# Gate and up products of two feed-forward layers by Strassen's algorithm, with down products in five steps between the pairs

## Chip, cores and metric

One Trainium2 chip, one core of it. The metric is the device time of one execution in microseconds; the kernel before takes 1113.04 us (median of 3 runs, 1112.74 to 1113.41).

## What is computed

A decoder layer in float32 for 512 tokens of width 1024: a feed-forward layer, a token mixer with two kinds of attention, a second feed-forward layer, a last normalisation. The change concerns the feed-forward layers alone:

```python
def swiglu(x, w_gate, w_up, w_down):
    return (jax.nn.silu(x @ w_gate) * (x @ w_up)) @ w_down

x = x + 0.5 * swiglu(rms_norm(x, ffn1_norm), ffn1_w_gate, ffn1_w_up, ffn1_w_down)
...
x = x + 0.5 * swiglu(rms_norm(x, ffn2_norm), ffn2_w_gate, ffn2_w_up, ffn2_w_down)
```

The inner width is 2816, which is 22 blocks of 128.

## The kernel before

Activations lie transposed: 8 tiles of 128 channels by 512 tokens. To keep float32 accuracy, every operand of a product is split in a high part (rounded to the matmul's format by a cast on ScalarE, `whi`) and a low part (what is left, by a subtraction on VectorE, `wlo`). A product then takes three matmuls for each 128 channels: low weights by high activations, high by high, high weights by low activations (`mm3`, L109 to L112). `split` (L98 to L104) makes the two parts of a block of weights in three rotating buffers each; `load` (L92) brings a block on SP's queue into two rotating buffers of 1 MB (`wraw`).

`ffn_up` (L310) goes through the 22 inner blocks. For each it makes a gate and an up product, `gemm` (L114): 8 channel tiles x 3 matmuls with 512 tokens each, into one PSUM bank. `finish` (L313) multiplies both by the row factors of the norm (`Rb`), applies silu on ScalarE, multiplies, and splits the result in `hh` and `hl`. All 22 pairs are kept. The down product of the first layer (L381 to L394) comes after the last block: for four pairs of output tiles, over all 22 blocks. That of the second (L930 to L932, with tokens on the output's partitions) also follows after all blocks, into all eight banks at once. Rotary tables (`rope_table`, L354) are made beside five steps of the first layer and stay in SBUF.

Within an engine, instructions run in the order that the program has; this order is set by a scheduler from the program's dependences, except at the very start. TensorE does its steps in the order of the code.

Of the kernel before, what the change touches and what calls it, by code (L numbers as in the profile page):

```python
# [56 lines left out]
def hybrid_layer_kernel(ctx: ExitStack, tc: tile.TileContext, x, positions,  # L57
# [11 lines left out]
    wraw = ctx.enter_context(tc.tile_pool(name="wraw", bufs=2))  # L69
# [16 lines left out]
    cmask = const.tile([P, T], F32, name="cmask")  # L86
    pool.memset(cmask, 0.0)
    pool.affine_select(out=cmask[:, T - P:T], in_=cmask[:, T - P:T], compare_op=ALU.is_ge, fill=-BIG,
                       base=0, pattern=[[-1, P]], channel_multiplier=1)

# [1 line left out]
    def load(view, eng=None):  # L92
        _, a, b = view.shape
        t = wraw.tile([P, a, b], F32, name="raw", tag="raw")
        (eng or nc.sync).dma_start(out=t, in_=view)
        return t
# [98 lines left out]
    xgp = xg_stack.enter_context(tc.tile_pool(name="xgp", bufs=KT))  # L195
    ffn1_stack = ExitStack()
    xpool = ffn1_stack.enter_context(tc.tile_pool(name="xpool", bufs=1))
    work = ffn1_stack.enter_context(tc.tile_pool(name="work", bufs=2))
    xt = [xpool.tile([P, T], F32, name=f"xt{k}") for k in range(KT)]

    def gain_split(src, gain):
        xh = xgp.tile([P, T], F32R, name="xh", tag="xh")
        xl = xgp.tile([P, T], F32R, name="xl", tag="xl")
        act.activation(xh, src, AF.Copy, scale=gain)
        vec.scalar_tensor_tensor(out=xl, in0=src, scalar=gain, in1=as_f32(xh), op0=ALU.mult, op1=ALU.subtract)
        return xh, xl
# [5 lines left out]
    tbl = ExitStack()  # L212
    tcs = tbl.enter_context(tc.tile_pool(name="tcs", bufs=1, side="right"))
    tbl_a = ExitStack()
    tqk = tbl_a.enter_context(tc.tile_pool(name="tqk", bufs=1, side="right"))

    with tc.tile_pool(name="xnat", bufs=1) as xnp:
# [11 lines left out]
        # keeps the tensor engine's clock up until the first operands are there  # L229
        warm = xnp.tile([P, T], BF16, name="warm")  # L230
        vec.memset(warm, 0.0)
        with tc.manual_schedule(engines={EN.PE, EN.Activation, EN.DVE}):
            ps_first = [bank(), bank()]
            first_w = [[xnp.tile([P, KT, P], F32R, name=f"first_{n}{j}") for n in ("hi", "lo")] for j in range(2)]
            xg = []
# [13 lines left out]
            def split_x(*ks):  # L249
                for k in ks:  # L250
                    xg.append(gain_split(tps[k], gain("ffn1", k)))
# [9 lines left out]
            def keep_x(*ks):  # L261
                for k in ks:
                    act.copy(xt[k], tps[k])
# [37 lines left out]
    def sumsq_add(work, acc, k, src):  # L301
        if k == 0:
            vec.tensor_tensor(out=acc, in0=src, in1=src, op=ALU.mult)
        else:
            sq = work.tile([P, T], F32, name="sq", tag="sq")
# [4 lines left out]
    def ffn_up(work, hp, w_gate, w_up, xg, r, first=None, extra=None):  # L310
        hs = []

        def finish(ps_g, ps_u):  # L313
            g = work.tile([P, T], F32, name="g", tag="g")
            u = work.tile([P, T], F32, name="u", tag="u")
            vec.tensor_tensor(out=g, in0=ps_g, in1=Rb, op=ALU.mult)  # L316
            act.activation(g, g, AF.Silu)
            vec.tensor_tensor(out=u, in0=ps_u, in1=Rb, op=ALU.mult)  # L318
            vec.scalar_tensor_tensor(out=g, in0=g, scalar=0.5, in1=u, op0=ALU.mult, op1=ALU.mult)
            hh = hp.tile([P, T], F32R, name="hh", tag="hh")  # L320
            hl = hp.tile([P, T], F32R, name="hl", tag="hl")
            act.copy(hh, g)
            vec.tensor_tensor(out=hl, in0=g, in1=as_f32(hh), op=ALU.subtract)
            hs.append((hh, hl))

        f = 0 if first is None else 1
        while f < FT:
            if extra is not None:
                extra(f)
            n = 1 if f % 2 else 2  # L330
            raw_g = load(kview(w_gate, f * P, (f + n) * P))
            raw_u = load(kview(w_up, f * P, (f + n) * P))
            for s in range(n):
                ps_g, ps_u = (bank("tp"), bank("sc")) if (f + s) % 2 else (bank(), bank())
                gemm(ps_g, split(raw_g[:, :, s * P:(s + 1) * P]), kcols, xg)
                if r is not None:
                    set_R(r)
                    r = None
                gemm(ps_u, split(raw_u[:, :, s * P:(s + 1) * P]), kcols, xg)
                if first is not None:  # L340
                    finish(*first)
                    first = None
                finish(ps_g, ps_u)
            f += n
        return hs

# [1 line left out]
    rc = const.tile([P, 20], F32, name="rc")  # L348
    pool.dma_start(out=rc, in_=rope_const)
    tables = [(tqk if j < 3 else tcs).tile([P, T], F32, name=f"table{j}") for j in range(5)]  # L350
    t_even, t_odd, t_kr, t_cos, t_sin = tables

    # rotary tables, one for each of a few steps of the first layer
    def rope_table(f):  # L354
        j = f // 2 - 2
        if f % 2 or not 0 <= j < 5:
            return
        c = rc[:, 4 * j:4 * j + 4]
        t = tables[j]
        pos = work.tile([P, T], I32, name="pos", tag="sq")  # L360
        pool.dma_start(out=pos, in_=positions[0].partition_broadcast(P))
        a = work.tile([P, T], F32, name="ang", tag="g")
        kk = work.tile([P, T], F32, name="kk", tag="u")
# [9 lines left out]
        act.activation(t, a, AF.Sin)  # L373
        vec.tensor_scalar(out=t, in0=t, scalar1=c[:, 2:3], scalar2=c[:, 3:4], op0=ALU.mult, op1=ALU.add)

    with tc.tile_pool(name="h1", bufs=FT) as hp:
        hs = ffn_up(work, hp, ffn1_w_gate, ffn1_w_up, xg, r0, ps_first, rope_table)
        xg = []
        acc = work.tile([P, T], F32, name="acc", tag="u")
        wd = ffn1_w_down[0].rearrange("(a p) n -> p a n", p=P)  # L380
        for n2 in range(KT // 2):  # L381
            pss = [bank(), bank()]
            for f0, f1 in ((0, 8), (8, 16), (16, 22)):
                raw = load(wd[:, f0:f1, n2 * 256:(n2 + 1) * 256])
                for s in range(2):
                    wh, wl = split(raw[:, :, s * P:(s + 1) * P])
                    for f in range(f0, f1):
                        mm3(pss[s], wh[:, f - f0, :], wl[:, f - f0, :], hs[f][0], hs[f][1], f == 0, f == FT - 1)
            for s in range(2):
                k = n2 * 2 + s  # L390
                vec.tensor_tensor(out=xt[k], in0=xt[k], in1=pss[s], op=ALU.add)
                pool.dma_start(out=x1d[k], in_=xt[k])
                xg.append(gain_split(xt[k], gain("mix", k)))
                sumsq_add(work, acc, k, xt[k])  # L394
# [6 lines left out]
    off = dict(cq=0, ckv=256, kr=384, dq=416, dk=928, dv=1440, gm=1952, gd=2976)  # L401
    mix = ExitStack()
# [44 lines left out]
    # decoupled key: columns [key, swapped key] in high parts, then in low parts  # L447
# [19 lines left out]
    # sums the four row groups and repeats the sum in each  # L467
# [17 lines left out]
    # differential values, put by in DRAM  # L485
# [16 lines left out]
    # minus lambda  # L502
# [543 lines left out]
```

## Time and profile before

| what | value |
|---|---|
| runs | 1112.74, 1113.04, 1113.41 us |
| profiled execution: span from its first to its last instruction | 1111.0 us |
| TensorE busy, share of the span | 1097.5 us, 99% |
| VectorE busy | 608.0 us, 55% |
| ScalarE busy | 414.1 us, 37% |
| moved by DMA | 130.10 MB, mean 117 GB/s |

The profile is that of one execution. What the runs have above its span (2.0 us for their median) lies before its first and after its last instruction, together with the spread of the runs. A busy time is the time in which an engine has at least one instruction; matmuls overlap each other, so 99% says that TensorE has work nearly always, not how fast it goes through it.

### The profile page before, as it was taken

How to read it: one execution, taken by the hardware profiler on the slowest of the kernel's cores; microseconds unless marked ns; L12 is line 12 of the kernel's file. 1: busy time of each engine (PE TensorE's matmuls, PEld its weight loads, DVE VectorE, ACT ScalarE, POOL GpSimd, SP SyncE). 2: the span in 40 equal slices, each digit the busy share in tenths (PEclk: the TensorE clock that was granted, in tenths of full speed). 3: DMA queues.
4: the chain of work that ended last, by engine and by line, in shares of the span. 5: the costliest groups of instructions: out<-in, count | busy, mean ns of one | idle time of the engine just before them, and what ended most of it. 6: DMA issues, size and time to landing. Idle time of an engine off the chain costs nothing.

```text
span 1111.0 us, 12841 instructions
## 1 busy us (share of the span) xinstructions
PE 1097.5 (99%) x4972; PEld 898.0 (81%) x4972; DVE 608.0 (55%) x1143; ACT 414.1 (37%) x710; POOL 43.4 (4%) x48
## 2 busy tenths in 40 slices
PE   8999999999999999999999999999999999999997
PEld 6888888888888887888777788888888888888885
DVE  5666654442333567998488868554444444432223
ACT  5433333331222334666455534433222333221124
POOL 2000000000000100022000000000000000000003
PEclk9999999999999999999999999999999999999999
DMA  7324323323323415442766247333223323323221
GB/s 220 106 92 130 107 76 102 125 77 105 121 93 119 123 48 152 119 128 81 254 198 188 87 148 235 119 95 114 76 81 125 99 76 111 116 95 114 76 76 76
DMA packets 112174, 130.10 MB, mean 117 GB/s; under 512 B 4038, under 2 KB 95344, under 8 KB 112112
## 3 DMA queue, kind: packets, MB, share of 16 engines
q1 hardware_dynamic: 103664, 111.32, 31.3%
q10 hardware_dynamic: 6944, 13.87, 3.8%
q0 software_dynamic: 1504, 4.09, 1.2%
q8 instruction: 39, 0.64, 0.2%
q14 instruction: 23, 0.19, 0.0%
HBM read 113.01 MB, written 15.73 MB: 116 GB/s over the span
## 4 chain that ended last, share of the span: by engine, by line
PE 96%; DVE 2%; DMA 1%; ACT 0%; issue 0%; SPq 0%; DVEq 0%; ACTq 0%
PE bank_gb L110 18%; PE bank_gb L112 18%; PE bank_gb L111 18%; PE bank_sc L112 4%; PE bank_sc L111 4%; PE bank_sc L110 4%; PE bank_tp L110 4%; PE bank_tp L111 4%; PE bank_tp L112 4%; PE bank_sc L930 1%; PE bank_sc L932 1%; PE bank_sc L931 1%; PE bank_sc L767 1%; PE bank_gb L930 1%; PE bank_tp L932 1%; PE bank_tp L930 1%
## 5 line engine op out<-in xcount | busy, mean ns | idle before, releaser
L102 ACT CAST whi<-raw 128x1024 fp32r<-128x1024 f32 (+1 forms) x183 | 183.8, 1006 | 514.5 <-PE bank_gb L112 271.6
L103 DVE TENSOR_TENSOR wlo<-raw,whi 128x1024 fp32r<-128x1024 f32 (+1 forms) x175 | 203.3, 1162 | 151.2 <-ACT whi L102 150.5
L110 PE MATMUL bank_gb<-xh,wlo 128*128 128x512 f32 x544 | 218.4, 401 | 0.0
L112 PE MATMUL bank_gb<-xl,whi 128*128 128x512 f32 x544 | 213.5, 392 | 0.0
L111 PE MATMUL bank_gb<-xh,whi 128*128 128x512 f32 x544 | 212.7, 391 | 0.0
L110 PEld LDWEIGHTS bank_gb<-xh,wlo 128*128 128x128 f32 x544 | 102.5, 188 | 23.3 <-issue 3.0
L112 PEld LDWEIGHTS bank_gb<-xl,whi 128*128 128x128 f32 x544 | 102.4, 188 | 22.3 <-issue 0.4
L111 PEld LDWEIGHTS bank_gb<-xh,whi 128*128 128x128 f32 x544 | 102.6, 189 | 19.3
L110 PE MATMUL bank_tp<-xh,wlo 128*128 128x512 f32 x184 | 71.8, 390 | 0.0
L111 PE MATMUL bank_tp<-xh,whi 128*128 128x512 f32 x184 | 71.6, 389 | 0.0
L112 PE MATMUL bank_tp<-xl,whi 128*128 128x512 f32 x184 | 71.6, 389 | 0.0
L110 PE MATMUL bank_sc<-xh,wlo 128*128 128x512 f32 x176 | 68.6, 390 | 0.0
L112 PE MATMUL bank_sc<-xl,whi 128*128 128x512 f32 x176 | 68.5, 389 | 0.0
L112 PE MATMUL bank_gb<-hl,whi 128*128 128x512 f32 x176 | 68.5, 389 | 0.0
L110 PE MATMUL bank_gb<-hh,wlo 128*128 128x512 f32 x176 | 68.5, 389 | 0.0
L111 PE MATMUL bank_sc<-xh,whi 128*128 128x512 f32 x176 | 68.5, 389 | 0.0
L111 PE MATMUL bank_gb<-hh,whi 128*128 128x512 f32 x176 | 68.5, 389 | 0.0
L318 DVE TENSOR_TENSOR u<-bank_sc,Rb 128x512 f32<-128x512 f32 x22 | 15.2, 691 | 63.1 <-PE bank_sc L112 63.1
L318 DVE TENSOR_TENSOR u<-bank_gb,Rb 128x512 f32<-128x512 f32 x22 | 15.2, 691 | 56.6 <-PE bank_gb L112 56.6
L589 DVE CUSTOM_DVE_ANT_0 bank_sc<-bank_sc,cmask 128x128 f32<-128x128 f32 (+3 forms) x64 | 31.5, 496 | 18.1 <-PE bank_sc L767 17.4
L316 DVE TENSOR_TENSOR g<-bank_tp,Rb 128x512 f32<-128x512 f32 x22 | 15.2, 691 | 46.8 <-PE bank_tp L112 46.8
L112 PEld LDWEIGHTS bank_tp<-xl,whi 128*128 128x128 f32 x184 | 34.6, 188 | 7.2
(396 smaller groups left out, 1845.3 us busy)
## 6 DMA issues: line engine op xcount, KB each, us to landing
raw<-in_ffn_w_gate_dram SPq DMA_DIRECT2D x21, 1024.0 KB
raw<-in_ffn_w_up_dram SPq DMA_DIRECT2D x21, 1024.0 KB
raw<-in_ffn_w_down_dram SPq DMA_DIRECT2D x19, 1024.0 KB
raw<-in_w_in_dram SPq DMA_DIRECT2D x11, 1024.0 KB
raw<-in_w_in_dram SPq DMA_DIRECT2D x8, 512.0 KB
raw<-in_w_out_dram SPq DMA_DIRECT2D x4, 1024.0 KB
raw<-in_ffn_w_down_dram SPq DMA_DIRECT2D x4, 768.0 KB
xn<-in_x_dram SPq DMA_DIRECT2D x4, 512.0 KB
```

The source lines that it names most:

```text
L102: act.copy(hi, src)
L103: (eng or vec).tensor_tensor(out=lo, in0=src, in1=as_f32(hi), op=ALU.subtract)
L110: pe.matmul(ps, wl, xh, start=start, stop=False)
L111: pe.matmul(ps, wh, xh, start=False, stop=False)
L112: pe.matmul(ps, wh, xl, start=False, stop=stop)
L316: vec.tensor_tensor(out=g, in0=ps_g, in1=Rb, op=ALU.mult)
L318: vec.tensor_tensor(out=u, in0=ps_u, in1=Rb, op=ALU.mult)
L589: vec.tensor_tensor_reduce(out=ps[:, 0:n], in0=ps[:, 0:n], in1=cmask[:, T - n:T], op0=ALU.add, op1=ALU.min, scale=-scale, scalar=3e38, acc ...
L767: pe.matmul(ps[:, 0:n], qa[rs, s, qs], kl[rs, 0:n], start=False, stop=True)
L930: pe.matmul(ps, hh[:, ts], wl[:, cs], start=first, stop=False)
L931: pe.matmul(ps, hh[:, ts], wh[:, cs], start=False, stop=False)
L932: pe.matmul(ps, hl[:, ts], wh[:, cs], start=False, stop=(f == FT - 1))
```

## The change

The first two pairs of inner blocks (four blocks) stay as they were. For the other nine pairs, `strassen_pair` takes the 256 inner columns of a pair (two blocks, for gate and for up), the 1024 channels (even and odd tiles) and the 512 tokens (two halves) as a product of 2 x 2 blocks, and makes it with seven products of blocks (in Winograd's form) in place of eight. One of the seven has 4 channel tiles, 256 tokens, and two groups g (gate and up): 2 x 4 x 3 matmuls with 256 columns. Three sums of it accumulate in one bank, `a`, which is copied out (`keep`) between the products. Sums of weights (`s1`, `s2` and two made in place) come on VectorE for every pair. Sums of activations (`T1` to `T4`) come once for each layer: `early` beside the last plain products, and `late`, which writes normalised operands over the tiles that the plain products read. For these, `xhat` holds the normalised activations in float32.

```diff
+    raws = [wraw.tile([P, RAW], F32, name="raw")]
+    turns = [0, 0]
+    def space(a, b):
+        n = 0 if len(raws) > 1 else 1
+        j, turns[n] = turns[n], 1 - turns[n]
+        flat = raws[0][:, j * RAW // 2:j * RAW // 2 + a * b] if n else raws[j][:, 0:a * b]
+        return flat.rearrange("p (a b) -> p a b", a=a)
...
+        def put(self, name, src):
+            hi, lo = self.t[name]
+            act.copy(hi, src)
+            vec.tensor_tensor(out=lo, in0=src, in1=as_f32(hi), op=ALU.subtract)
...
+        def late(self):
+            for name, (i, j) in (("B11", (0, 0)), ("T1", (0, 1)), ("B21", (1, 0)), ("B22", (1, 1))):
+                self.put(name, self.B[i][j])
+    def strassen_pair(work, sums, ops, raw, G):
+        A = [[raw[:, :, j::2, (1 - i) * P:(2 - i) * P] for j in range(2)] for i in range(2)]
...
+        def product(ps, w, t, first):
+            (wh, wl), (th, tl) = w, ops.t[t]
+            for g in range(2):
+                o = ps[:, g * HT:(g + 1) * HT]
+                for k in range(KT // 2):
...
+                    pe.matmul(o, wl[:, g, k, :], th[:, k, :], start=first and n, stop=False, skip_group_check=True)
+                    pe.matmul(o, wh[:, g, k, :], th[:, k, :], start=False, stop=False, skip_group_check=True)
+                    pe.matmul(o, wh[:, g, k, :], tl[:, k, :], start=False, stop=last, skip_group_check=True)
...
+        product(a, split(A[0][0]), "B11", True)
+        p1 = keep(a, "p1")
+        s1 = new("s1")
+        vec.tensor_tensor(out=s1, in0=A[1][0], in1=A[1][1], op=ALU.add)
+        s2 = new("s2")
+        vec.tensor_tensor(out=s2, in0=s1, in1=A[0][0], op=ALU.subtract)
+        c = bank8()
+        product(c, split(s1), "T1", True)
+        p5 = keep(c, "p5")
+        product(a, split(s2), "T2", False)
+        u2 = keep(a, "u2")
+        b = bank8()
+        product(b, split(A[0][1]), "B21", True)
+        vec.tensor_tensor(out=C[:, 1, :], in0=b, in1=p1, op=ALU.add)
+        vec.tensor_tensor(out=A[1][0], in0=A[0][0], in1=A[1][0], op=ALU.subtract)
+        product(a, split(A[1][0]), "T3", False)
+        u3 = keep(a, "u3")
+        vec.tensor_tensor(out=C[:, 0, :], in0=u3, in1=p5, op=ALU.add)
+        vec.tensor_tensor(out=A[0][0], in0=A[0][1], in1=s2, op=ALU.subtract)
+        product(c, split(A[0][0]), "B22", False)
+        vec.tensor_tensor(out=C[:, 2, :], in0=c, in1=u2, op=ALU.add)
+        product(a, split(A[1][1]), "T4", False)
...
+        ops.late()
+        for m in range(PLAIN, NPAIR):
...
+            strassen_pair(work, sums, ops, load_pair(w_gate, w_up, m), G)
+            hs[m] = hidden(work, hp, G)
+            if m % 2 == 0 and m + 2 < NPAIR:
+                down([(n, hs.pop(n)) for n in (m - 2, m - 1)])
```

The down product is cut in five steps in both layers: after the pairs 2, 4, 6 and 8 one for two earlier pairs (`down1`, `down2`: 96 matmuls of 512 columns, whose result VectorE adds to x), and at the end one for the last three pairs, which in the second layer is the ending of before with six blocks in place of 22. Two weight buffers of 2 MB take turns, one pair or one down step in each. The rotary tables are written to DRAM from POOL's queue and read back on ScalarE's queue (`tabd`, L529 and L594 of the changed kernel). The number of matmuls grows by 2 x 9 x (168 - 96) = 1296.

On TensorE, within a plain block of the first layer (waits in brackets, names of buffers without numbers), before:

```order
L110 MATMUL bank_gb<-xh,wlo 128x512 [waits DVE_49]
L111 MATMUL bank_gb<-xh,whi 128x512 [waits Activation_49]
L112 MATMUL bank_gb<-xl,whi 128x512
L110 MATMUL bank_gb<-xh,wlo 128x512
```

and at two places of the second Strassen pair of the first layer, now: around the start of its second product (`bank_gb` is `a`, `bank_sc` is `c`),

```order
L406 MATMUL bank_gb<-xl_129,whi 128x256
L404 MATMUL bank_sc<-xh_128,wlo 128x256 [waits DVE_49]
L405 MATMUL bank_sc<-xh_128,whi 128x256 [waits Activation_49]
L406 MATMUL bank_sc<-xl_129,whi 128x256
```

which waits for the two halves of its weights at two matmuls, as before, and around the start of its third, which accumulates onto `a`:

```order
L406 MATMUL bank_sc<-xl_129,whi 128x256
L404 MATMUL bank_gb<-t2h,wlo 128x256 [waits DVE_49,Activation_49]
L405 MATMUL bank_gb<-t2h,whi 128x256
L406 MATMUL bank_gb<-t2l,whi 128x256
```

Here the first matmul waits for VectorE (the low half) and for ScalarE (the copy of the bank) at once, and the second for nothing.

On VectorE, in the first layer where the first Strassen pair begins. The first row needs the end of the last plain product; `xl` are the low halves of B11, T1, B21 and B22, `s_603` is s1 and `s_605` s2. Before, at a like place (the end of block 3), it had:

```order
L318 TENSOR_TENSOR u<-bank_sc,Rb 128x512
L366 TENSOR_SCALAR kk<-ang,rc 128x512
L319 SCALAR_TENSOR_TENSOR g<-g,u 128x512
L367 TENSOR_SCALAR kk<-kk 128x512
L103 TENSOR_TENSOR wlo<-raw,whi 128x1024
L323 TENSOR_TENSOR hl<-g,hh 128x512
```

and now:

```order
L350 TENSOR_TENSOR u<-bank_sc,Rb 128x512
L370 TENSOR_TENSOR xl_129<-xhat_314,xh_128 128x4x256
L351 SCALAR_TENSOR_TENSOR G<-g,u 128x512
L370 TENSOR_TENSOR xl_129<-xhat_314,xh_128 128x4x256
L370 TENSOR_TENSOR xl_131<-xhat_314,xh_130 128x4x256
L341 TENSOR_TENSOR hl<-G,hh 128x1024
L370 TENSOR_TENSOR xl_131<-xhat_314,xh_130 128x4x256
L420 TENSOR_TENSOR s_605<-s_603,raw 128x1024
L110 TENSOR_TENSOR wlo<-s_603,whi 128x1024
L429 TENSOR_TENSOR raw<-raw 128x8x128
L110 TENSOR_TENSOR wlo<-s_605,whi 128x1024
```

The low half of s1, with which the second product of the pair begins, has moved behind eight other instructions that follow the end of the last plain product.

The same place in the second layer (`s_7539` is s1, `s_7541` is s2), now:

```order
L110 TENSOR_TENSOR wlo<-s_7539,whi 128x1024
L350 TENSOR_TENSOR u<-bank_sc,Rb 128x512
L370 TENSOR_TENSOR xl_6813<-x2t,xh_6812 128x4x256
L351 SCALAR_TENSOR_TENSOR G<-g,u 128x512
L370 TENSOR_TENSOR xl_6813<-x2t,xh_6812 128x4x256
L370 TENSOR_TENSOR xl_6815<-x2t,xh_6814 128x4x256
L341 TENSOR_TENSOR hl<-G,hh 128x1024
L370 TENSOR_TENSOR xl_6815<-x2t,xh_6814 128x4x256
L110 TENSOR_TENSOR wlo<-s_7541,whi 128x1024
```

Here the low half of s1 stands ahead of the end of the last plain product, and that of s2 behind the four operands.

## Rows read from the trace of the kernel before

**Rows 1.** The page, busy time, share of the span and instructions of each engine.
```profile
PE 1097.5 (99%) x4972; PEld 898.0 (81%) x4972; DVE 608.0 (55%) x1143; ACT 414.1 (37%) x710; POOL 43.4 (4%) x48
```

**Rows 2.** The page, chain that ended last, shares of the span by engine.
```profile
PE 96%; DVE 2%; DMA 1%; ACT 0%; issue 0%; SPq 0%; DVEq 0%; ACTq 0%
```

**Rows 3.** Window, length, busy PE, PEld, DVE, ACT, POOL, clock, DMA, GB/s.
```profile
30.00:377.00 347.00, 347.00 (x1535) 287.20 (x1533) 173.83 (x234) 107.02 (x134) 8.05 (x15) 1.00 0.32 104
```

**Rows 4.** Timeline of the first layer (start, duration, engine, line, operation).
```profile
99.69 0.39 PE L110 MATMUL bank_sc<-xh,wlo 128*128 128x512 f32 x1
...
105.13 0.39 PE L110 MATMUL bank_gb<-xh,wlo 128*128 128x512 f32 x1
```

**Rows 5.** Timeline of TensorE where the mixer's scores begin.
```profile
441.88 0.33 PE L110 MATMUL bank_sc<-kth,ql 128*128 128x256 f32 x1
442.05 0.28 PE L111 MATMUL bank_sc<-kth,qh 128*128 128x256 f32 x1
442.17 0.28 PE L112 MATMUL bank_sc<-ktl,qh 128*128 128x256 f32 x1
442.29 0.34 PE L110 MATMUL bank_sc<-kth,ql 128*128 128x384 f32 x1
```

**Rows 6.** Timeline of a chain of matmuls with 256 columns and their loads.
```profile
576.05 1.02 PEld L793 LDWEIGHTS bank_pv<-dv,pt 128*128 128x128 f32 x8
...
576.07 1.20 PE L793 MATMUL bank_pv<-dv,pt 128*128 128x256 f32 x8
...
576.99 0.19 PEld L766 LDWEIGHTS bank_sc<-ka,qa 128*128 128x128 f32 x1
```

**Rows 7.** Timeline of eight loads for matmuls of one column.
```profile
742.28 0.97 PEld L187 LDWEIGHTS bank_sc<-ones,acc 128*128 128x128 f32 x8 [0.28 <-DVE acc L307]
```

**Rows 8.** Instructions of L110 on the load side of TensorE's queue: ns min/median/max.
```profile
L110 PEldq EVENT_SEMAPHORE  x11: 51/51/3815, 8.3 to 797.3; - x11
```

**Rows 9.** Groups by line and shape, VectorE: xcount, busy us, mean ns, idle before.
```profile
L103 DVE TENSOR_TENSOR wlo<-raw,whi 128x1024 fp32r<-128x1024 f32 x151 | 184.6, 1223 | 117.4 <-ACT whi L102 116.8
L319 DVE SCALAR_TENSOR_TENSOR g<-g,u 128x512 f32<-128x512 f32 x44 | 30.5, 692 | 4.6 <-ACT g L317 1.1
...
L103 DVE TENSOR_TENSOR wlo<-raw,whi 128x768 fp32r<-128x768 f32 x8 | 7.7, 958 | 33.7 <-ACT whi L102 33.7
...
L205 DVE SCALAR_TENSOR_TENSOR xl<-xk,gc,xh 128x512 fp32r<-128x512 f32 x8 | 6.0, 745 | 0.0
...
L692 DVE TENSOR_TENSOR ptl<-bank_tp,pth 128x256 fp32r<-128x256 f32 x8 | 3.3, 416 | 1.2 <-ACT pth L691 1.2
```

**Rows 10.** The same view, ScalarE.
```profile
L102 ACT CAST whi<-raw 128x1024 fp32r<-128x1024 f32 x159 | 167.2, 1053 | 459.4 <-PE bank_gb L112 216.7 <-PE bank_sc L112 80.8 <-PE bank_tp L112 70.2
```

**Rows 11.** Timeline of TensorE after a wait in the mixer.
```profile
445.64 0.50 PE L110 MATMUL bank_sc<-kth,ql 128*128 128x512 f32 x1 [2.19 <-ACT e L591]
...
446.67 0.63 PE L110 MATMUL bank_gb<-xh,wlo 128*128 128x512 f32 x1
447.09 0.63 PE L111 MATMUL bank_gb<-xh,whi 128*128 128x512 f32 x1
```

**Rows 12.** Columns as in rows 3: the stretch after that wait.
```profile
445.60:449.40 3.80, 3.76 (x10) 2.92 (x11) 3.54 (x13) 3.06 (x9) 0.00 (x0) 0.57 0.01 2
```

**Rows 13.** DMA issues: count, KB each, median us to landing.
```profile
x1d<-xt POOLq DMA_DIRECT2D x8, 256.0 KB, 2.3
```

**Rows 14.** Columns as in rows 3: a stretch at the start.
```profile
8.00:12.00 4.00, 3.67 (x15) 2.99 (x16) 3.07 (x5) 2.92 (x6) 0.00 (x0) 0.66 1.08 334
```

**Rows 15.** Timeline at the start: cast of block 1's gate weights, its first product.
```profile
20.11 1.12 ACT L102 CAST whi<-raw 128x1024 fp32r<-128x1024 f32 x1
...
23.83 0.50 PE L110 MATMUL bank_tp<-xh,wlo 128*128 128x512 f32 x1
```

**Rows 16.** Groups by shape, VectorE, 50 to 110 us: operations of a rotary table.
```profile
L365 DVE TENSOR_SCALAR ang<-ang,rc 128x512 f32<-128x512 f32 x3 | 1.4, 481 | 0.0
...
L374 DVE TENSOR_SCALAR table<-table,rc 128x512 f32<-128x512 f32 x2 | 1.1, 548 | 1.4 <-ACT table L373 1.4
```

More of the change, by code (lines that the diff above doesn't have):

```diff
@@ L304, in sumsq_add @@
         else:
-            sq = work.tile([P, T], F32, name="sq", tag="sq")
+            sq = work.tile([P, T], F32, name="sq", tag="w", bufs=6)
             act.activation(sq, src, AF.Square)
             vec.tensor_tensor(out=acc, in0=acc, in1=sq, op=ALU.add)
[L310 to L335, printed above, removed]
@@ new lines, in hybrid_layer_kernel, with bank8, halves, hidden @@
+    HT = T // 2
+    EIGHT = ("gb", "sc", "tp", "gb", "sc", "tp", "sc", "pv")
+    turn8 = iter(lambda n=[0]: EIGHT[(n.__setitem__(0, n[0] + 1) or n[0] - 1) % 8], None)
+    def bank8():
+        return bank(next(turn8))
+    def halves(ps):
+        return ps.rearrange("p (g t) -> p g t", g=2)
+    def hidden(work, hp, G):
+        hh = hp.tile([P, 4, HT], F32R, name="hh")
+        hl = hp.tile([P, 4, HT], F32R, name="hl")
+        act.copy(hh, G)
+        vec.tensor_tensor(out=hl, in0=G, in1=as_f32(hh), op=ALU.subtract)
+        return hh, hl
@@ new lines, in load_pair, with ffn_up @@
+    def load_pair(w_gate, w_up, m):
+        raw = space(2 * KT, 2 * P).rearrange("p (g k) c -> p g k c", g=2)
+        for g, w in enumerate((w_gate, w_up)):
+            nc.sync.dma_start(out=raw[:, g], in_=kview(w, 2 * m * P, (2 * m + 2) * P))
+        return raw
+    NPAIR = FT // 2
+    PLAIN = 2
+    def ffn_up(pools, hp, w_gate, w_up, X, xsrc, xhat, gname, r, first, extra, down):
+        work, ttp, sums = pools
+        xg = x_parts(X)
+        hs = {}
+        ops = None
+        for m in range(PLAIN):
+            G = new_G(work)
+            raw = None
+            for s in range(2):
+                f = 2 * m + s
+                if first is not None and f == 0:
+                    continue
+                if first is not None and f == 1:
+                    one = space(2 * KT, P).rearrange("p (g k) c -> p g k c", g=2)
+                    for g, w in enumerate((w_gate, w_up)):
+                        nc.sync.dma_start(out=one[:, g], in_=kview(w, P, 2 * P))
+                    cols = [one[:, g] for g in range(2)]
+                else:
+                    if raw is None:
+                        raw = load_pair(w_gate, w_up, m)
+                    cols = [raw[:, g, :, s * P:(s + 1) * P] for g in range(2)]
+                ps_g, ps_u = (bank("tp"), bank("sc")) if s else (bank(), bank())
+                gemm(ps_g, split(cols[0]), kcols, xg)
@@ L372, in rope_table @@
         vec.tensor_scalar(out=a, in0=a, scalar1=-PI_LO, scalar2=None, op0=ALU.max)
[L373 to L380, printed above, removed]
-        for n2 in range(KT // 2):
-            pss = [bank(), bank()]
-            for f0, f1 in ((0, 8), (8, 16), (16, 22)):
-                raw = load(wd[:, f0:f1, n2 * 256:(n2 + 1) * 256])
+        act.activation(kk, a, AF.Sin)
```

240 lines of the change are left out of this document (180 added, 60 removed).

## Prediction

> **What bounds the kernel now.** I read the page's busy times first: TensorE is busy 1097.5 of 1111.0 us, VectorE 608.0, ScalarE 414.1 [rows 1]. The chain that ended last is TensorE for 96% [rows 2]. Cut into stages, 30 to 377 us (the first feed-forward layer) has TensorE busy without a gap at the full clock, VectorE busy 173.8 of 347 us [rows 3]. So there the time is the number of matmuls times their pitch (start to start), and only a change of these two, or a gap that they do not have now, moves the end. In the timeline 24 starts of 512-column matmuls lie 5.44 us apart, from 99.69 to 105.13 us, over a change of bank and of weights: a pitch of 0.2267 us [rows 4]. A matmul's own duration there, 0.39 us, is longer than its pitch and is of no use for a sum.
>
> **What a Strassen pair saves.** Before, two blocks of gate and up are four products of 24 matmuls of 512 columns: 96 x 0.2267 = 21.76 us. The change makes seven products of 24 matmuls of 256 columns: 168 matmuls, of which each loads its own 128 columns of weights as before. In columns this is 7/8; the question is the pitch at 256. The scores of the mixer show it: from L111 to L112 and to the next matmul 0.12 us each (442.05, 442.17, 442.29) [rows 5]. A chain of eight with 256 columns shows the same from the loads: eight loads take 1.02 us, the last of them 0.19, so (1.02 - 0.19) / 7 = 0.1187 us [rows 6]. Eight loads beside matmuls of a single column take 0.97 us, so 0.111 us [rows 7]: that is a floor that the load sets, and 256 columns lie just above it. I take 0.12, read from starts: 168 x 0.12 = 20.16 us, a gain of 1.60 us a pair. With nine pairs in each of two layers: **18 x 1.60 = 28.8 us off**. The ends: 32.8 us at 0.1187, and a loss at 0.131 (a rival below).
>
> At 512 columns a load has 0.11 us to spare; at 256 it has almost none, so what holds up TensorE's queue shows. A second wait on a matmul is an instruction of its own, 51 ns (11 of them at L110) [rows 8]; in the new order the three products of a pair that accumulate onto an old bank have two waits. 18 x 3 x 0.051 = **2.8 us on**. From below this is nothing; from above every one of the 126 products pays the 0.05 us by which the first of three matmuls in [rows 5] (441.88 to 442.05) exceeds 0.12: 6.3 us. I take the row of the second wait, since the plain loop's single waits show no such instruction.
>
> **VectorE in a pair.** It has seven low halves, four sums and one hidden low half of 1024 elements, 12 x 1.223; three C sums at 0.69; one product of 768, 0.96; one of 256, 0.42 [rows 9]: 18.2 us of 20.16. ScalarE has eight casts of 1.053 [rows 10], four copies of half the size and two activations: at most 14 x 1.053 = 14.7 us. Three buffers of split weights let both run two products (5.8 us) ahead of TensorE, so in the steady run I charge nothing; the cover is the 2 us a pair by which VectorE is the shorter, and if it goes, the excess is paid. A down step is the same 96 matmuls of 512 columns in another cut, 21.76 us, with four splits (4.9 us) and eight additions of 0.69 us (5.5) on VectorE: it gives back 11 us of slack. Its additions into x (64 more in the two layers) cost nothing beside that.
>
> **The start of the first pair** is where the change adds waits. The operands B11, T1, B21, B22 overwrite the plain products' activations, so they can only be written when the last plain product has ended. In the first layer VectorE is late there already: between the end of product u of block 2 and that of block 3 (4 x 24 matmuls, 21.8 us) its queue has 12 instructions of 1024 (14.7 us), six xhat products of 0.745 (4.5) and six of 0.69 (4.1) [rows 9]: 23.3 us, so 1.5 us late. Behind it stand, ahead of the low half of s1, with which product 2 begins: u and G (1.4 us), four operands, hl, s2 and that low half itself (7 x 1.223 = 8.6). Product 2 can start 11.5 us after the last plain product, where product 1 would let it start after 24 x 0.12 = 2.9: **8.6 us on**. Nothing else is for TensorE to do, since its order is fixed. After a wait of 2.19 us the trace has TensorE at a pitch of 0.42 (446.67 to 447.09) [rows 11], in 3.8 us at a mean granted clock of 0.57, so mostly at the lower level of 1.2 GHz [rows 12]: 3.8 x 0.43 = 1.6 us lost, and I charge it once here: **1.6 on**. In the second layer the low half of s1 stands ahead of the operands, and VectorE comes with time to spare. Product 1 waits for B11's low half (u 0.69, then 1.22, less its first two matmuls and the hand-over: 1.8 us), and product 3 for that of s2: two of 0.69 and six of 1.223 after the end, 8.7 us, where it is due at 1.8 + 5.8 = 7.6, so 1.2 us with the hand-over. **3.0 on, 3.4** with a part of a clock fall whose rest the second wait hides. Together the starts cost 13.6 us; from below 10.1 (no delay, no clock fall), from above 17 if both gaps in both layers bring the clock down.
>
> **Small parts.** The rotary tables now go through DRAM: five writes on POOL's queue and five reads on ScalarE's. A read on ScalarE waits for its write (such a write of 256 KB lands 2.3 us after issue [rows 13]), and the splits queue behind it; the order puts each read one to three instructions behind the table's sine, and the two products that the splits are ahead cover the rest. Nothing, with 0 to 1 us each as bounds. SP's queue now has 1.57 MB more ahead of block 1's gate weights: at 334 GB/s [rows 14], 4.7 us. Before, that block's cast began at 20.11 us and its product at 23.83 [rows 15]; it may land a little later than that cast now, with about 1 us of cover: nothing, at worst 2 us. A pair's 2.1 MB take 6.3 us at that rate, in steps of 20, so both buffers keep up. The mixer and the ending keep their work and their order of stages: nothing, 1 us either way.
>
> **The sum** on the profiled execution: 1111.0 - 28.8 + 2.8 + 13.6 = 1098.6 us of span. The median of the runs, 1113.0, lies 2.0 us above that span, so the forecast is **1100.6 us**, 1.1% less. A difference over 0.2% (2.2 us) can be told from none by a measurement of this kernel.
>
> **The rivals.**
> - *Cheap start*: the pitch is 0.1187 throughout (gain 32.8), no queue cost, starts at 10.1: 1113.0 - 22.7 = 1090.3 us. For it speaks the chain of loads; against it VectorE's count of instructions before the first pair.
> - *Slower: the pitch at 256 columns.* The same chain of eight, read by its matmuls, takes 1.20 us with the last at 0.28: (1.20 - 0.28) / 7 = 0.131 us [rows 6]. Then a pair is 168 x 0.131 = 22.0 us, nothing is gained (0.25 x 18 = 4.5 lost), and queue and starts come on top: 1113.0 + 4.5 + 16.4 = 1134 us. It decides from the pitch at which 18 x (21.76 - 168 p) = 16.4, p = 0.124. Against it: the start of that first matmul is recorded 0.02 us after its load begins, which no other is, and the scores' starts say 0.12.
> - *VectorE sets the pairs with a table.* A table is seven operations of at most 0.48, two of 0.69 and one of 0.55, some 5.3 us [rows 9, 16]: 18.2 + 5.3 = 23.5 in a pair of 20.2. Five pairs pay 3.3 us: 1100.6 + 16.5 = 1117 us. Against it: the order takes up to three sums of the next pair into the down steps, where VectorE has slack, which leaves such a pair some 19.8.
> - *Loads do not overlap.* By the rows, a matmul that had to wait for its load would cost the 0.111 us of a load [rows 7] and a stream of (0.2267 - 0.111) x n / 512: at 256 columns 0.169, so 28.4 us a pair and 1113 + 119 + 16 = 1248 us. It fails at 256 columns, where the rows show 0.12. The Trainium skill, "TensorE: Matmul & The Clock Gate", in its part on packing small matmuls, says that a weight load overlaps running matmuls only when it goes to other row groups; by that rule, with all 128 rows in use, this rival would hold. The trace does not agree: 0.12 us instead of 0.169.
>
> **How the numbers follow.** Forecast 0.60 (1095 to 1106), cheap start 0.20, tables 0.08, pitch 0.11, loads 0.01. Range 1086 to 1115: all of the forecast, 0.16 of the cheap start, half of the tables, 0.80. The tables need not cost their full price, so their 0.08 lie between the forecast and 1117. Faster by over 0.2% (under 1110.8): the first two and 0.01 of the tables, 0.81; within: 0.04 of the tables; slower (over 1115.2): pitch, loads and 0.03 of the tables, 0.15.
>
> **What would show it.** Matmuls of the pairs 0.12 us apart, a pair in 20.2 to 20.5 us; a gap of 5 to 6 us on TensorE ahead of the first layer's second Strassen product, released by a low half on VectorE, and about 3 us in two parts in the second layer; VectorE busy some 90% in the pairs. A pitch of 0.125 or more, TensorE waiting for low halves in the later pairs, or waits on loads of weights would prove the forecast wrong.

## The result, and the profile after

The changed kernel takes 1097.41 us (median of 4 runs, 1096.59 to 1098.98) against 1113.22 us before: a ratio of 0.9857, 95% interval 0.9843 to 0.9871, so 1.4% less. The forecast was 1100.6 us. The profiled execution has a span of 1095.4 us, and the median of the runs lies 2.0 us above it, as it did before. The page's busy times and its chain that ended last, for the changed kernel:

```profile
PE 1072.3 (98%) x6268; PEld 936.7 (86%) x6268; DVE 815.4 (74%) x1331; ACT 513.8 (47%) x828; POOL 52.2 (5%) x53
...
PE 92%; DVE 4%; DMA 2%; ACT 1%; issue 1%; SPq 0%; DVEq 0%; ACTq 0%
```

Against [rows 1, 2]: TensorE has 1296 matmuls more and is busy 25 us less, VectorE rises from 608.0 to 815.4 us, and the chain is still TensorE's, 92% in place of 96%. VectorE's share of it rises from 2% to 4%; its longest new pieces are the starts of the first Strassen pairs (from 58.25 us and from 781.65 us on, below).

**Where the time went.** Four points that both kernels have cut the span in the same stages. Of the timeline of TensorE, before: the row factors of the first layer, the last matmul of its down product, the last of the output projection, the last of all:

```profile
29.41 1.05 PE L180 MATMUL bank_sc<-ident,r 128*128 128x128 f32 x8
...
372.82 0.39 PE L112 MATMUL bank_gb<-hl,whi 128*128 128x512 f32 x1
...
738.23 0.40 PE L112 MATMUL bank_gb<-ml,whi 128*128 128x512 f32 x1
...
1103.34 0.40 PE L932 MATMUL bank_gb<-lwh,hl 128*128 128x512 f32 x1
```

and the same four now:

```profile
29.80 1.16 PE L187 MATMUL bank_sc<-ident,r 128*128 128x128 f32 x8 [1.71 <-DVE r L181]
...
367.30 0.39 PE L119 MATMUL bank_tp<-hl,whi 128*128 128x512 f32 x1
...
734.57 0.40 PE L119 MATMUL bank_gb<-ml,whi 128*128 128x512 f32 x1
...
1088.01 0.40 PE L1124 MATMUL bank_gb<-lwh,hl 128*128 128x512 f32 x1
```

| stage | before | after | difference |
|---|---|---|---|
| to the first layer's row factors | 29.41 | 29.80 | +0.4 |
| first layer | 343.41 | 337.50 | -5.9 |
| mixer and projections | 365.41 | 367.27 | +1.9 |
| second layer | 365.11 | 353.44 | -11.7 |
| after the last matmul | 7.66 | 7.39 | -0.3 |

These add up to -15.6 us, the difference of the spans. By the pitch of a pair (below) each layer gains 9 x 1.605 = 14.4 us; the first gives more than half of it back, nearly all of that in one place.

**A Strassen pair.** Timeline of TensorE over the pairs 3 and 4 of the first layer, from the first matmul of the one to the first of the down step behind the other, with the starts of the third and fourth product of pair 3 between:

```profile
108.25 0.28 PE L404 MATMUL bank_gb<-xh,wlo 128*128 128x256 f32 x1
...
114.00 0.28 PE L404 MATMUL bank_gb<-t2h,wlo 128*128 128x256 f32 x1
...
116.88 0.28 PE L404 MATMUL bank_tp<-xh,wlo 128*128 128x256 f32 x1
...
148.56 0.40 PE L117 MATMUL bank_sc<-hh,wlo 128*128 128x512 f32 x1
```

Two pairs last 40.31 us, so one takes 20.155: 168 matmuls at 0.1200. All eight such couples of the two layers (two pairs between two down steps) measure 40.31 or 40.32. The third product accumulates on an old bank and has two waits; it takes 116.88 - 114.00 = 2.88 us, no more than the others. The second waits are there, on the load side of TensorE's queue (count, ns min/median/max), and cost nothing that a product's time would show:

```profile
L404 PEldq EVENT_SEMAPHORE  x57: 51/51/51, 54.0 to 1049.8; - x57
```

VectorE is not the bound of a pair. Window, length, busy PE, PEld, DVE, ACT, POOL, clock, DMA, GB/s, of those two pairs and of the down step behind them:

```profile
108.25:148.56 40.31, 40.31 (x337) 40.31 (x336) 30.88 (x39) 21.94 (x27) 1.09 (x2) 1.00 0.29 91
...
148.56:170.35 21.79, 21.79 (x99) 18.03 (x97) 20.86 (x29) 6.19 (x7) 1.07 (x2) 1.00 0.65 194
```

It is busy for 30.88 of 40.31 us, 77%, with a rotary table's operations among them; in the down step it is busy 96%, since it finishes the pair and makes sums of the next one there.

**The start in the first layer.** Timeline of TensorE and VectorE to the first down step. The first two lines are VectorE before the last plain product ends, the third is the last matmul of the plain blocks:

```profile
36.49 0.69 DVE L350 TENSOR_TENSOR u<-bank_sc,Rb 128x512 f32<-128x512 f32 x1
...
56.55 1.23 DVE L418 TENSOR_TENSOR s<-raw 128x1024 f32<-128x1024 f32 x1
...
57.82 0.39 PE L119 MATMUL bank_sc<-xl,whi 128*128 128x512 f32 x1
...
58.25 0.69 DVE L350 TENSOR_TENSOR u<-bank_sc,Rb 128x512 f32<-128x512 f32 x1 [0.47 <-PE bank_sc L119]
...
58.85 1.22 DVE L370 TENSOR_TENSOR xl<-xhat,xh 128x1024 fp32r<-128x1024 f32 x1
...
60.13 0.39 PE L406 MATMUL bank_gb<-xl,whi 128*128 128x256 f32 x1 [1.18 <-DVE xl L370]
...
62.86 1.22 DVE L341 TENSOR_TENSOR hl<-G,hh 128x1024 fp32r<-128x1024 f32 x1
...
65.13 1.22 DVE L420 TENSOR_TENSOR s<-s,raw 128x1024 f32<-128x1024 f32 x1
...
66.27 1.22 DVE L110 TENSOR_TENSOR wlo<-s,whi 128x1024 fp32r<-128x1024 f32 x1
...
67.63 0.36 PE L404 MATMUL bank_sc<-xh,wlo 128*128 128x256 f32 x1 [4.61 <-DVE wlo L110]
...
86.46 0.40 PE L117 MATMUL bank_gb<-hh,wlo 128*128 128x512 f32 x1
```

The last plain matmul's successor could start at 57.82 + 0.23 = 58.05, and the down step begins at 86.46: 28.4 us for a pair of 20.16, so 8.3 on. TensorE waits 0.24 us for the high half of B11 from ScalarE, 1.18 us for its low half, and 4.61 us for the low half of s1, which VectorE has started at 66.27, behind the end of the plain block (`hl`), four operands and s2. That is the place and the queue that the prediction named. VectorE was not late, though: from 36.49 us (`u` of block 2) it worked without a gap until 56.55 + 1.23 = 57.78, and then stood idle for 0.47 us ahead of `u` of block 3. Behind the wait the granted clock is halved for a while (columns as above):

```profile
69.00:70.00 1.00, 1.00 (x6) 1.00 (x6) 1.00 (x2) 0.00 (x0) 1.00 (x1) 0.50 0.00 0
...
72.00:73.00 1.00, 1.00 (x10) 1.00 (x10) 0.03 (x1) 0.73 (x2) 0.18 (x1) 1.00 0.00 0
```

Product 3 starts at 72.07 us, so product 2 takes 72.07 - 67.63 = 4.44 us in place of 2.88.

**The start in the second layer.** The same view there:

```profile
781.23 0.39 PE L119 MATMUL bank_sc<-xl,whi 128*128 128x512 f32 x1
...
782.80 0.39 PE L404 MATMUL bank_sc<-xh,wlo 128*128 128x256 f32 x1 [0.44 <-ACT xh L369]
...
789.90 0.36 PE L404 MATMUL bank_gb<-t2h,wlo 128*128 128x256 f32 x1 [0.84 <-DVE wlo L110]
...
804.36 0.39 PE L1122 MATMUL bank_sc<-wlo,hh 128*128 128x512 f32 x1
```

804.36 - 781.23 - 0.23 - 20.16 = 2.7 us on, in four waits of 0.2 to 0.8 us, two of them for high halves from ScalarE. TensorE begins product 2 (`bank_sc`) before product 1 is done, so its steps do not stand in the order of the code here, and the clock stays at its upper level.

### The profile page after: what moved, and what is told of

Same layout as the page of the kernel before. It is cut to its first block, busy times and chain, and to the rows that moved or that the text cites. A ratio compares the mean times of both kernels' runs of the same rounds, so it can differ in the third digit from the quotient of the medians.

```text
span 1095.4 us, 15774 instructions
## 1 busy us (share of the span) xinstructions
PE 1072.3 (98%) x6268; PEld 936.7 (86%) x6268; DVE 815.4 (74%) x1331; ACT 513.8 (47%) x828; POOL 52.2 (5%) x53
## 4 chain that ended last, share of the span: by engine, by line
PE 92%; DVE 4%; DMA 2%; ACT 1%; issue 1%; SPq 0%; DVEq 0%; ACTq 0%
PE bank_gb L117 9%; PE bank_gb L119 8%; PE bank_gb L118 8%; PE bank_sc L404 4%; PE bank_sc L405 4%; PE bank_sc L406 4%; PE bank_gb L404 3%; PE bank_gb L405 3%; PE bank_gb L406 3%; PE bank_tp L406 3%; PE bank_tp L405 3%; PE bank_sc L118 3%; PE bank_tp L404 3%; PE bank_sc L117 3%; PE bank_sc L119 3%; PE bank_tp L118 2%
## 5 line engine op out<-in xcount | busy, mean ns | idle before, releaser
L109 ACT CAST whi<-raw 128x1024 fp32r<-128x1024 f32 (+1 forms) x124 | 123.3, 996 | 120.2 <-PE bank_gb L119 31.1
L110 DVE TENSOR_TENSOR wlo<-raw,whi 128x1024 fp32r<-128x1024 f32 (+1 forms) x116 | 133.3, 1150 | 52.3 <-ACT whi L109 52.1
L110 DVE TENSOR_TENSOR wlo<-fraw,whi 128x1024 fp32r<-128x1024 f32 x77 | 92.1, 1197 | 48.8 <-ACT whi L109 48.7
L109 ACT CAST whi<-fraw 128x1024 fp32r<-128x1024 f32 x77 | 79.2, 1029 | 83.9 <-PE bank_gb L119 30.6
L117 PE MATMUL bank_gb<-xh,wlo 128*128 128x512 f32 x256 | 106.2, 415 | 0.0
L119 PE MATMUL bank_gb<-xl,whi 128*128 128x512 f32 x256 | 101.0, 395 | 0.0
L118 PE MATMUL bank_gb<-xh,whi 128*128 128x512 f32 x256 | 100.4, 392 | 0.0
L404 PE MATMUL bank_sc<-xh,wlo 128*128 128x256 f32 x224 | 64.2, 287 | 5.0 <-DVE wlo L110 4.6
L405 PE MATMUL bank_sc<-xh,whi 128*128 128x256 f32 x224 | 64.1, 286 | 0.0
L406 PE MATMUL bank_sc<-xl,whi 128*128 128x256 f32 x224 | 64.1, 286 | 0.0
L110 DVE TENSOR_TENSOR wlo<-s,whi 128x1024 fp32r<-128x1024 f32 x36 | 44.0, 1222 | 15.7 <-ACT whi L109 15.1
L783 DVE CUSTOM_DVE_ANT_0 bank_sc<-bank_sc,cmask 128x128 f32<-128x128 f32 (+3 forms) x64 | 31.5, 496 | 18.2 <-PE bank_sc L961 17.4
```

Of the source, the lines that this page charges most:

```text
L109: act.copy(hi, src)
L110: (eng or vec).tensor_tensor(out=lo, in0=src, in1=as_f32(hi), op=ALU.subtract)
L117: pe.matmul(ps, wl, xh, start=start, stop=False)
L118: pe.matmul(ps, wh, xh, start=False, stop=False)
L119: pe.matmul(ps, wh, xl, start=False, stop=stop)
L404: pe.matmul(o, wl[:, g, k, :], th[:, k, :], start=first and n, stop=False, skip_group_check=True)
```

## The experiments

### The order of the start alone

In both layers VectorE's and ScalarE's work for the first Strassen pair is put in another order; nothing is added or left out.

```diff
         a = bank8()
-        product(a, split(A[0][0]), "B11", True)
-        p1 = keep(a, "p1")
+        w1 = split(A[0][0])
         s1 = new("s1")
...
+        late("B11")
+        late("T1")
+        w2 = split(s1)
         s2 = new("s2")
...
+        product(a, w1, "B11", True)
+        p1 = keep(a, "p1")
         c = bank8()
-        product(c, split(s1), "T1", True)
+        product(c, w2, "T1", True)
...
         b = bank8()
+        late("B21")
         product(b, split(A[0][1]), "B21", True)
...
         vec.tensor_tensor(out=A[0][0], in0=A[0][1], in1=s2, op=ALU.subtract)
+        ended()
+        late("B22")
         product(c, split(A[0][0]), "B22", False)
```

`late` writes one operand and `ended` does u, G and the hidden activations of the last plain block; both do nothing in the other pairs.

> Only the order of the start of the first Strassen pair is changed, in both layers: the split of s1 and the sum s2 come ahead of the operands B21 and B22, each of these two just ahead of the product that reads it, and the end of the last plain block (u, G, hidden) behind the fifth product. Theory (VectorE's queue sets the start): in the changed kernel the pair of the first layer takes 28.0 us and that of the second 22.5, where others take 20.16; product 2 no longer waits, the clock does not fall, and what is left is the wait of product 1 for the low half of B11, some 1.5 us a layer: 6 to 8.5 us less in all, 1089 to 1091.5 us. Rival (the overwriting itself sets it, since no operand can be written before the last plain product has ended): the wait of 4.6 us turns into waits of the products 1, 3 and 4 of the same sum, and the time stays within 2 us of 1097.4.

Measured: 1090.86 us (5 runs), ratio 0.9792, interval 0.9779 to 0.9806. Timeline of TensorE in the first layer, from the last plain matmul on:

```profile
58.53 0.39 PE L119 MATMUL bank_sc<-xl,whi 128*128 128x512 f32 x1
...
60.94 0.39 PE L412 MATMUL bank_gb<-xl,whi 128*128 128x256 f32 x1 [1.28 <-DVE xl L376]
...
82.43 0.40 PE L117 MATMUL bank_gb<-hh,wlo 128*128 128x512 f32 x1
```

The start costs 82.43 - 58.53 - 0.23 - 20.16 = 3.5 us in place of 8.3, and 1.3 in place of 2.7 in the second layer. Product 2 waits no more, so VectorE's queue, and not the overwriting of the operands, held it. Two parts of the theory fell. In the second layer what is left is not the low half of B11 but two waits of 0.23 and 0.44 us for high halves from ScalarE. And in the first the clock drops here too, behind waits of 0.24 and 1.28 us for B11 alone (windows, columns as above); the matmuls there start 0.21 us apart from 62.01 to 65.22 us, and from 65.40 on 0.12:

```profile
59.00:61.00 2.00, 0.57 (x3) 0.36 (x3) 2.00 (x3) 2.00 (x4) 0.00 (x0) 1.00 0.02 4
...
62.00:63.00 1.00, 1.00 (x7) 1.00 (x6) 1.00 (x2) 1.00 (x2) 0.00 (x0) 0.50 0.00 0
```

### The same without a wait for B11

To the order above comes a place of its own for B11, for the first pair (a buffer of the hidden activations that is not yet in use), so that it is split before the last plain product ends. T4's low half comes behind s1, and the ordering of loads of the next experiment is in it too.

```diff
+        b11 = [hp.tile([P, 4, HT], F32R, name=nm) for nm in ("hh", "hl")]
...
             self.put("T2", t2)
+            self.put("B11", B[0][0])
...
         product(a, w1, "B11", True)
+        late("B11")
```

Here `late("B11")` issues two copies on POOL's queue to the old place, for the later pairs.

> The two orders of before (the start of the first Strassen pair; the second layer's first weights behind the output projection's) and, for that first pair, B11 in tiles of its own (a buffer of the hidden activations that is still free), split before the last plain product ends; POOL's queue copies it to its later place afterwards. T4's low half comes behind s1. Theory (what was left at the start, 3.5 us in the first layer and 1.3 in the second, is the wait for B11 and the fall of the clock behind it): TensorE runs through from the last plain product into product 1; at most 0.5 us a layer at product 2, no fall of the clock; 1090.9 - 1.7 (loads) - 2.5 to 4.5 (starts) = 1084.7 to 1086.7 us. Rival (VectorE is full in the stretch before, so B11's earlier split makes the last plain block or product 2 late by as much): the clock falls all the same, 1088 to 1090 us.

Measured: 1086.56 us (4 runs), ratio 0.9763, interval 0.9748 to 0.9777. Timeline of TensorE in the first layer:

```profile
58.04 0.28 PE L420 MATMUL bank_gb<-hh,wlo 128*128 128x256 f32 x1
...
65.54 0.39 PE L420 MATMUL bank_gb<-t2h,wlo 128*128 128x256 f32 x1 [1.40 <-DVE wlo L112]
...
80.04 0.40 PE L119 MATMUL bank_gb<-hh,wlo 128*128 128x512 f32 x1
```

and the second:

```profile
775.08 0.28 PE L420 MATMUL bank_gb<-hh,wlo 128*128 128x256 f32 x1
...
795.23 0.39 PE L1158 MATMUL bank_sc<-wlo,hh 128*128 128x512 f32 x1
```

In the second layer the first pair takes 20.15 us, like any other: nothing is left. In the first it takes 22.0; B11 and s1 come in time, and the one wait of 1.40 us is for the low half of s2 at product 3. The clock stays up through it:

```profile
64.00:67.00 3.00, 1.60 (x14) 1.46 (x13) 3.00 (x4) 1.70 (x3) 0.00 (x0) 1.00 0.00 0
```

The time lies inside the theory's range; the 0.5 us a layer were too little for the first layer, too much for the second. That the time lies in the range is in part luck: the range takes 1.7 us off for the order of the loads, which the next experiment does not bear out. The starts alone explain 1.7 + 1.3 = 3.0 of the 4.3 us between the two medians; where the rest comes from is not shown.

### The loads at the end of the mixer

The mixer's 1.9 us were the largest cost that the prediction had not seen. In the profile two waits of 0.2 and 0.35 us at 680 and 684 us, for a gate behind a late load of weights, lie in the stretch where it is lost, and the second layer's first 2 MB of weights now stand ahead of that load on SP's queue. The edit is one ordering:

```diff
+            if m == 0 and w_gate is ffn2_w_gate:
+                tc.add_manual_dep(d.ins, loads[-1].ins.name, ...)
```

> One ordering is added: the load of the second layer's first pair of weights (2 MB on SP's queue) comes behind the loads of the output projection, where in the changed kernel it stands ahead of the last weights of the second attention projection. Theory (the mixer's 1.85 us over the kernel before are this queue): the two waits of TensorE at 680 and 684 us go, 1.0 to 1.8 us less, 1095.6 to 1096.4 us. Rival (the 1.85 us come from the rotary tables that are now read back from DRAM, or from the shared slots of the weight buffers): no change beyond 0.4 us.

Measured: 1095.25 us (4 runs), ratio 0.9838, interval 0.9825 to 0.9852, and the two waits were gone from the profile. Since this is close to what two executions can differ by, the changed kernel and this one were run again on one chip:

> The changed kernel once more, unchanged, on the same chip as the next run, so that the two can be set against each other: 1096.5 to 1098.5 us, with TensorE's two waits near 680 and 684 us.

> The one ordering of the earlier run (second layer's first weights behind the output projection's) once more, against the changed kernel on the same chip. Theory (the two waits of TensorE at the end of the mixer are the queue, on every execution): 1.0 to 2.0 us less than the changed kernel in the medians. Rival (the gain seen in the profile is a matter of one execution, since the weights' transfers themselves are now and then late): under 0.5 us.

Measured: 1097.0 us (ratio 0.9851, interval 0.9835 to 0.9868) and 1095.92 us (0.9836, 0.9822 to 0.9851). The medians are 1.1 us apart and the intervals overlap. The profile decides against the theory: in the repeat of the unchanged kernel the waits are not there, and the stage between the two points lasts 733.69 - 367.98 = 365.7 us, as before the change:

```profile
367.98 0.39 PE L119 MATMUL bank_tp<-hl,whi 128*128 128x512 f32 x1
...
733.69 0.40 PE L119 MATMUL bank_gb<-ml,whi 128*128 128x512 f32 x1
```

In the repeat with the ordering it lasts 366.3, and in the version with B11's own place, which has the ordering as well, 367.3. In both of these TensorE waits at another place instead, in the output projection. Timeline of TensorE in the repeat with the ordering:

```profile
690.78 0.50 PE L121 MATMUL bank_gb<-ml,whi 128*128 128x512 f32 x1 [0.36 <-DVE ml L1075]
```

and in the version with B11's own place:

```profile
685.65 0.50 PE L121 MATMUL bank_gb<-ml,whi 128*128 128x512 f32 x1 [1.21 <-DVE ml L1107]
```

So the mixer's part differs by up to 2 us from one execution to the next, and it is neither shown to belong to the change nor to the order of these loads. The first 30 us behave the same: the row factors come at 29.6 to 31.1 us in the profiles of the changed kernel, its repeat and these versions.

### No Strassen pair at all

All eleven pairs are plain blocks, with the new buffers, the tables by way of DRAM and the five-step down products. Normalised operands and sums of activations are not made.

```diff
-    PLAIN = 2
+    PLAIN = NPAIR
```

> All eleven pairs stay plain blocks, with the new weight buffers, the tables by way of DRAM and the down product in five steps; normalised operands and sums of activations are not made. Theory: the Strassen pairs alone give 18 x 1.605 = 28.9 us, their starts take 11.0 back, and everything else in the change (down steps, tables, buffers) costs only the 2 us seen in the mixer and at the start: 1097.4 + 28.9 - 11.0 = 1115.3 us. Rival (the down steps or the loads between the pairs carry a cost or a gain of their own): over 1118 or under 1112 us.

Measured: 1114.98 us (10 runs), ratio 1.0019, interval 1.0010 to 1.0028. In the timeline the down step of the first layer is 96 matmuls in 21.76 us:

```profile
80.56 0.39 PE L117 MATMUL bank_gb<-hh,wlo 128*128 128x512 f32 x1
...
102.32 0.39 PE L117 MATMUL bank_gb<-xh,wlo 128*128 128x512 f32 x1
```

That is the pitch of the single down product of before, so cutting it in five is free, as forecast. In the second layer a step takes 22.31 us, 0.232 a matmul, which is the pitch of the single one of before too (528 starts in 122.48 us). The Strassen pairs with their starts are worth 1114.98 - 1097.41 = 17.6 us, where the profile's terms give 28.9 - 11.0 = 17.9.

### Half the columns again

All matmuls of the Strassen pairs but 14 of 168 (the first of low weights in each product and group) take 128 of their 256 columns, so the results lack those parts of the products, half of each bank's columns (the expectation says three quarters, by mistake).

```diff
-                    pe.matmul(o, wh[:, g, k, :], th[:, k, :], ...)
+                    pe.matmul(o[:, c], wh[:, g, k, :], th[:, k, c], ...)
```

> In the Strassen products every matmul but the one at the first channel tile of low weights takes 128 of its 256 columns, so three quarters of each bank's tokens get nothing more; 16 of 168 matmuls of a pair (14 by the count of products and groups) keep 256. Theory (a load of weights sets a floor of 0.11 us, just under the 0.12 at 256 columns): a pitch of 0.110 to 0.112, a pair in 18.5 to 18.9 us, 22 to 30 us less, 1068 to 1075 us. Rival (no floor: the pitch is columns at 2.4 GHz plus 13 ns, so 0.067 us): VectorE's some 16.6 us set the pair, 60 us less or more, under 1040 us.

Measured: 1153.58 us (one run), slower by 56 us than with twice the columns. Neither theory had that. Where TensorE is not disturbed the floor is as expected; in the pairs 9 and 10 of the first layer the pitch is (386.93 - 349.28) / 336 = 0.112 us:

```profile
349.28 0.28 PE L405 MATMUL bank_tp<-xh,wlo 128*128 128x256 f32 x1
...
386.93 0.45 PE L117 MATMUL bank_gb<-hh,wlo 128*128 128x512 f32 x1
```

But a wait is now far dearer, in this one execution. Windows, columns as above, over the pairs 7 and 8 and over 9 and 10:

```profile
252.00:296.00 44.00, 44.00 (x302) 40.46 (x301) 33.19 (x40) 15.54 (x18) 1.07 (x2) 1.00 0.36 114
296.00:300.00 4.00, 1.38 (x10) 1.24 (x10) 3.96 (x6) 2.71 (x4) 0.00 (x0) 0.93 0.00 0
300.00:325.00 25.00, 25.00 (x119) 25.00 (x119) 11.73 (x13) 7.71 (x10) 0.54 (x1) 0.50 0.33 106
...
349.00:386.90 37.90, 37.90 (x338) 37.82 (x338) 26.93 (x28) 21.00 (x26) 0.00 (x0) 1.00 0.25 79
```

From 252 to 296 us all is well; then TensorE waits 2.6 us, and from 300 to 325 us it works without a gap at a clock of 0.50 (pitch 0.21), up to the next matmuls with 512 columns and some 4 us into them. A pair takes 18.8 us without such a wait, 26.2 (mean of a couple, with one wait in it) otherwise; the first pairs of the layers, with the waits of the start, take 39.9 and 35.4. The wait itself shows where the cover of the changed kernel ends. Timeline of ScalarE and TensorE:

```profile
297.30 1.04 ACT L340 CAST hh<-G 128x1024 fp32r<-128x1024 f32 x1 [2.92 <-DVE G L443]
...
298.78 0.56 ACT L411 COPY p<-bank_tp 128x512 f32<-128x512 f32 x1
...
299.39 0.57 PE L405 MATMUL bank_tp<-t2h,wlo 128*128 128x256 f32 x1 [2.62 <-ACT p L411]
```

The copy of bank `tp` stands on ScalarE behind the cast of the hidden activations, which has waited 2.92 us for VectorE; VectorE was at the operations of a rotary table. It happens in the couples of pairs with tables alone (three of them), not in the couple 9 and 10 nor in the later ones of the second layer. So by this one trace VectorE does set a pair with a table once TensorE needs only 18.8 us for it, and at 20.16 it does not.

### Two buffers of split weights

```diff
-    wspl = ctx.enter_context(tc.tile_pool(name="wspl", bufs=3))
+    wspl = ctx.enter_context(tc.tile_pool(name="wspl", bufs=2))
```

> The changed kernel with two buffers of split weights in place of three, for all products. Theory (the third buffer is the cover of the pairs: with two, the split of a product can only begin when the product two before it has ended, and cast 1.05, low half 1.22 and two hand-overs must fit into the 2.88 us of the one between, on engines that have other work in their queues): waits for low halves in most products of the pairs, 0.3 to 1 us each, so 38 to 126 us more, and the clock may fall behind them. Rival (one product ahead is enough): within 5 us of 1097.4.

Measured: 1127.3 us (4 runs), ratio 1.012, interval 1.0103 to 1.0137, so 30 us more than the changed kernel: between the two expectations, and neither. A product takes 2.97 to 3.05 us in place of 2.88 in the timeline, and in the first layer's couples up to 1.2 us are lost ahead of a third product to its low half. The 16 later pairs lose some 20 us together, the two first pairs 6.8, and the rest is lost outside the pairs; the clock stays at its upper level in the couples. The third buffer, which the kernel before has as well, is worth nearly twice the gain of the change.

## Why the prediction was right, step by step

| step | forecast, us | measured, us |
|---|---|---|
| 18 pairs at a pitch of 0.12 | -28.8 | 18 x (21.76 - 20.155) = -28.9 |
| second waits | +2.8 | 0 |
| start, first layer | +10.2 | +8.3 |
| start, second layer | +3.4 | +2.7 |
| start of the kernel, mixer, ending | 0 | +2.0, which differs between executions |

- **The pitch** was read from three starts in the scores of the mixer [rows 5], and it held to the last digit over the 2688 matmuls of the 16 pairs behind the first of each layer. The rival that read 0.131 from the durations of a chain [rows 6] fell, and so did the pitch of 0.1187 of the cheap start, of which only the free second waits came true. That matmuls with 256 columns lie just above the floor of a load [rows 7] is right too: at 128 columns the pitch stays at 0.112. Columns alone would give 0.067; from 512 to 256 columns the pitch falls by 0.2267 - 0.1200 = 0.1067 us, and 256 columns at 2.4 GHz are 0.1067, so above the floor a matmul costs its columns and 13 ns. The sentence of the Trainium skill ("TensorE: Matmul & The Clock Gate", part on packing small matmuls) by which a load overlaps only with other row groups does not, taken by itself, hold for this stream. The trace has 0.12 us with all rows in use, where the prediction had worked out 0.169 for a stream without overlap.
- **The second waits** are the step that failed in kind. The row of 51 ns [rows 8] was real and there are 57 of them; but a product with two waits takes 2.88 us like one with a single wait. The likely reason, argued and not shown, is that they pass in the load side's queue while earlier matmuls still run. What a queue's instruction lasts is not by itself a cost.
- **The start in the first layer** was right in its place and its cause, VectorE's queue in front of s1's low half, which the order of instructions showed and the first experiment proved: 1097.4 to 1090.9 us by order alone. Its size was 1.9 us too high. Of that 1.5 us is one term: VectorE's count of 23.3 us for the 21.8 before it used durations. The same 24 instructions took 21.3 us, from 36.49 to 57.78, so VectorE was 0.47 us early in place of 1.5 late. Those of 1024 elements that stand in a row start 1.14 us apart (three from 62.86 to 66.27) where each lasts 1.22. The forecast also put the whole delay ahead of product 2; 1.4 us of waits stood ahead of and within product 1. The fall of the clock, put in at 1.6 us, measured 4.44 - 2.88 = 1.56.
- **The second layer** had the waits at the places named (0.23 us for B11's low half, 0.84 for that of s2) and two more for high halves from ScalarE (0.24 and 0.44), which the forecast did not have; together 2.7 in place of 3.4 us. The clock did not fall there, which the forecast had charged in part.
- **VectorE in a pair** was put at 18.2 of 20.16 us and some 90%; it is 77%, mostly since the down steps take over work of the pairs: of the couple's 24 operations of 1024 elements only 17 start between 108.25 and 148.56 us. That it is no bound at 20.16, tables included, was right; the run with 128 columns shows that a table's pair is bound by it below that. The three buffers were named as the cover, rightly: without the third, 30 us are gone.
- **Small parts** at nothing: a down step of the first layer takes 21.79 us, 0.03 more than 96 matmuls of before, and the second layer's are free too. The mixer's 1.9 us were no part of the forecast's 1 us either way, and the repeat shows them to come and go.

The forecast was 3.2 us too high. In the terms of the table the second waits (2.8) and the starts (2.6) were too dear, and 2.0 that it had at nothing stands against them, which leaves 3.4; the rest is in the roundings and in what executions differ by. That the unforeseen 2.0 us hid part of the excess is luck; the large term and the place of the waits are not.

## What to carry to other kernels

Read a pitch from starts, not from durations, on every engine: that made the large term exact on TensorE, and its neglect on VectorE made most of the error at the first start. Where a scheme changes its operands in the middle of a stream, count what stands on the helping engine between the last old product and the first new one; here order alone was worth more than a third of what the whole change gained. And before matmuls are made narrower, look at what a single wait then costs, not only at the pitch.

## What the hardware showed that was not expected

- In the changed kernel a wait of 4.61 us was followed by a granted clock of 0.50, with a pitch of 0.21 us from 68.36 to 71.56 us. In the first experiment waits of 0.24 and 1.28 us were followed by the same, from 62.01 to 65.22 us. Waits of 0.24 and 1.18 us in the changed kernel, ahead of a product at a pitch of 0.12 and before the long one, were not followed by it, nor was the one of 1.40 us in the version with B11's own place. What tells these apart was not tried.
- In those two falls the clock rose again within the Strassen products of 256 columns. In the run with 128 columns TensorE worked without a gap at a clock of 0.50 from 300 to 325 us, and the clock rose only after matmuls of 512 columns had begun. There it also fell in the second layer's first pair, behind waits of 0.23 to 0.50 us, where the changed kernel's clock stayed up behind the like. This is one execution, and why is not shown.
- Two waits on one matmul cost nothing, in 48 products of the undisturbed pairs.
